# An attention mask carried in the score product's own rows, in a two-layer encoder

## The chip, the cores and the metric

The kernel runs on one core of a Trainium2 chip. The time is in device microseconds (us); it is the median of three runs. One launch computes the whole encoder for one sequence of 512 tokens.

## What is computed

The reference has two layers of the same build. Each adds to the stream x (512 x 1024) half of a SwiGLU feed-forward, then a mixing block, then half of a second feed-forward, and then it is normed. The mixing block has two groups side by side: latent attention with 8 heads, and a causal depthwise convolution of 31 taps over 512 channels; one output projection joins them. The part that the change touches is the attention's scores:

```python
CHUNK, Q_BLOCK, QK_DIM = 64, 128, 96
for i in range(s // Q_BLOCK):                       # 4 blocks of 128 queries
    qs, ks, vs = q[:, :, q0:q0 + 128], k[:, :, :k_end], v[:, :, :k_end]   # k_end = q0 + 128
    scores = einsum('bhqd,bhkd->bhqk', qs, ks) * QK_DIM ** -0.5
    allowed = (arange(k_end) // CHUNK)[None, :] <= ((q0 + arange(128)) // CHUNK)[:, None]
    probs = softmax(where(allowed, scores, -1e30))
    outs.append(einsum('bhqk,bhkd->bqhd', probs, vs))
```

Since a query block sees keys up to its own end only, just one corner of each block has to be masked: the first 64 queries of a block against the last 64 keys.

## The kernel before

**The stages of a layer.** Everything lies transposed, with features on the 128 partitions and the 512 tokens in the free dimension. The two feed-forwards and the projections are products of float32 operands that are split into a high and a low part, three products each (L144 to L146). The mixing block's attention and convolution run together in one stretch, here called the head stage: from 460 to 518 us in layer 0 and from 1370 to 1427 in layer 1 of the profiled execution.

**The attention.** For each head, `turn` (L615) transposes the queries and the keys of 96 features to tiles `qT` and `kT` of 512 columns; ScalarE scales the queries out of PSUM (L625), VectorE the keys (L630). `scores` (L633) makes four score products, one for each block of queries, of 128, 256, 384 and 512 keys (L646); behind each comes a mask product (L647), which adds `mrow` times `mneg` to the last 64 columns: `mrow` and `mneg` are bfloat16 tiles with one row that is not zero, 1 for the first 64 queries and -1e30. Then VectorE takes the maximum of each row (L648) and ScalarE the exponential with its sum (L652). `turn_p` (L656) transposes the probabilities (L667), and VectorE copies two of the three results out of PSUM and ScalarE one (L670). `values` (L673) makes the products with the values (L680). `turn_out` turns a pair of heads (L698).

**Order.** The heads are a pipeline that is written out by `ORDER = "t0s1p3v4o5"`: in each step a head is turned, the one before it makes its scores, and so on; two heads are turned ahead. The final place of an instruction on its engine is set by the framework's scheduler, which models when operands and buffers are there. Each engine then runs its own list in order.

**The convolution.** `CONV = "DAAD"` gives the four channel groups of the convolution to engines: two groups are one VectorE instruction for each tap (`cv`, L734), and in the other two ScalarE makes a tap's product (`pr`, L738) and POOL adds it (`y`, L742). These fill the same stretch as the heads. When all four are done, POOL sums them (L756 to L758) in `t`, and TensorE's product `pm` (L760) takes their mean over the channels. So the mixing block goes on with what is late of the two groups.

**Buffers and loads.** `qT`, `kT` and the probabilities are tiles of a ring of 41 buffers of 128 x 512 (named `r`). Weights are loaded by SP's queue into `raw`, three buffers in turn (L129); a load waits on SP until its buffer is free, and SP runs its list in order. The eight pieces of the output projection `wout` are loaded this way in the head stage: four of them of the kind "sum" (ScalarE makes the negative, and a POOL transfer adds the weights to it, L134 and L135). Behind them stand, on SP, the loads `fr` of the second feed-forward's weights (`wgu`, L253).

Of the kernel before, what the change touches and what calls it, by code (L numbers as in the profile page):

```python
# [6 lines left out]

FP = mybir.dt.float32
FR = mybir.dt.float32r
BF = mybir.dt.bfloat16  # L10
I32 = mybir.dt.int32
AF = mybir.ActivationFunctionType
ALU = mybir.AluOpType
# [2 lines left out]
P = 128  # L16
D = 1024
S = 512
# [4 lines left out]
DN = 64  # L23
DR = 32
DQ = DN + DR
DV = 64
QL = 384
KVL = 256
# [37 lines left out]


@with_exitstack
def encoder_kernel(ctx: ExitStack, tc: tile.TileContext, xT, consts, vecs, rgain, wgu1, wd1,
                   wcv, wql, wkl, wuq, wkv, wout, wgu2, wd2, out):  # L70
    nc = tc.nc
    PSUM = bass.MemoryType.PSUM
    cpool = ctx.enter_context(tc.tile_pool(name="const", bufs=1))
# [8 lines left out]
    def nm(s):  # L82
        uid[0] += 1
        return f"{s}{uid[0]}"

    def slot(dt=FP, w=S):
        return ring.tile([P, w], dt, tag="r", name=nm("r"))

    def tmp(w=S, dt=FP):
        return tmps.tile([P, w], dt, tag="t", name=nm("t"))  # L90

    def bank():
        return psum.tile([P, S], FP, tag="ps", name=nm("ps"))

    def tiny(tag, w, dt=FP):
        return small.tile([P, w], dt, tag=tag, name=nm(tag))

    V, A, G, T = nc.vector, nc.scalar, nc.gpsimd, nc.tensor
# [3 lines left out]
    vec = cpool.tile([P, L, VN], FP, name="vec")  # L102
# [10 lines left out]
    V.memset(minus_half, -0.5)  # L113
    onesm = cpool.tile([P, P], FP, name="onesm")
    V.memset(onesm, 1.0 / CW)
    mrow = cpool.tile([P, P], BF, name="mrow")
    V.memset(mrow, 0.0)
    V.memset(mrow[0:1, 0:64], 1.0)
    mneg = cpool.tile([P, 64], BF, name="mneg")
    V.memset(mneg, 0.0)  # L120
    V.memset(mneg[0:1, :], -1e30)

    def vv(l, name):
        o, w = VOFF[name]
# [309 lines left out]
    def mix_body(kpool, l, gx, norm, done):  # L434
# [27 lines left out]
        ck = kpool.tile([P, NT, KW], FP, tag="ck", name=nm("ck"), bufs=1)  # L462
        q = kpool.tile([P, NT, H, DQ], FP, tag="q", name=nm("q"), bufs=1)
        kn = kpool.tile([P, NT, H, DQ], FP, tag="kn", name=nm("kn"), bufs=1)
        cq, wkl_, sk, ckc, ratio = (tiny(n, NT) for n in ("cq", "wkl", "sk", "ckc", "ratio"))
# [42 lines left out]
        def rope(v, tb, h):  # L508

            nt = v.shape[1]  # L510
            x1, x2 = v[:, :, :, 0:16], v[:, :, :, 16:32]
            m = []
            w = nt * h * 16
            s1, s2 = tmp(), tmp()
            for i, src in enumerate((x1, x2, x1, x2)):
                a = (s1, s2)[i // 2][:, i % 2 * w:(i % 2 + 1) * w]
                a = a.rearrange("p (t h j) -> p t h j", t=nt, h=h)
                V.tensor_tensor(a, src, tb[:, i, :, None, :].to_broadcast([P, nt, h, 16]), ALU.mult)
                m.append(a)
            V.tensor_tensor(x1, m[0], m[1], ALU.subtract)  # L520
            V.tensor_tensor(x2, m[2], m[3], ALU.add)
# [9 lines left out]
        def token_terms():  # L531


            vx = norm.st.ve
            V.tensor_scalar(cq, vx, EPS * EPS * DQ, None, ALU.mult)
            V.scalar_tensor_tensor(cq, stq.sums(), EPS * DQ / QL, cq, ALU.mult, ALU.add)
            V.tensor_scalar(wkl_, vx, EPS, None, ALU.mult)
# [3 lines left out]
            V.tensor_tensor(ckc, ckc, sspe, ALU.mult)  # L541
            V.scalar_tensor_tensor(ckc, ckc, EPS * DQ, wkl_, ALU.add, ALU.mult)
            V.tensor_tensor(ratio, rm, sk, ALU.mult)
            V.tensor_tensor(ratio, ratio, wkl_, ALU.mult)

        def queries():
            wq = [load_w(wuq[l, :, k * 768:(k + 1) * 768], 768, "uq") for k in range(3)]
            for t in range(NT):
# [17 lines left out]
                if t % 2:  # L566
                    rope(q[:, t - 1:t + 1, :, DN:DQ], tabs[0][:, :, t - 1:t + 1], H)
                    if not QFOLD:
# [49 lines left out]
        heads = [{} for _ in range(H)]  # L618

        def turn(h):  # L620
            ps = bank()
            for t in range(NT):
                T.transpose(ps[0:DQ, t * P:(t + 1) * P], q[:, t, h], ident)
            qT = slot()
            A.activation(qT[0:DQ], ps[0:DQ], AF.Copy, scale=gqs[0:DQ])  # L625
            ps = bank()
            for t in range(NT):
                order["turned"] = T.transpose(ps[0:DQ, t * P:(t + 1) * P], kn[:, t, h], ident).ins
            kT = slot()
            V.tensor_scalar(kT[0:DQ], ps[0:DQ], gk, None, ALU.mult)  # L630
            heads[h]["qk"] = qT, kT

        def scores(h):  # L633
            qT, kT = heads[h]["qk"]
            b01, b2, b3 = bank(), bank(), bank()
            if h % 2 == 0:
                heads[h]["sums"] = small.tile([P, NT, 2], FP, tag="sums", name=nm("sums"), bufs=3)
            sums = heads[h - h % 2]["sums"]
            mx = small.tile([P, NT], FP, tag="mx", name=nm("mx"), bufs=3)
            pi = []  # L640
            ps = [slot() for _ in range(3)]
            ps = [ps[0][:, 0:128], ps[0][:, 128:384], ps[1][:, 0:384], ps[2]]
            for i in range(NT):
                n = (i + 1) * P
                o = (b01[:, 0:128], b01[:, 128:384], b2[:, 0:384], b3)[i]
                T.matmul(o, qT[0:DQ, i * P:(i + 1) * P], kT[0:DQ, 0:n], start=True, stop=False)  # L646
                heads[h]["s"] = T.matmul(o[:, n - 64:n], mrow, mneg, start=False, stop=True).ins  # L647
                V.tensor_reduce(mx[:, i:i + 1], o, axis=AX.X, op=ALU.max, negate=True)  # L648
                p = ps[i]
                if QFOLD:  # L650
                    V.tensor_tensor(mx[:, i:i + 1], mx[:, i:i + 1], scqs[i][:, h:h + 1], ALU.mult)
                A.activation(p, o, AF.Exp, bias=mx[:, i:i + 1], scale=scqs[i][:, h:h + 1] if QFOLD else 1.0,  # L652
                             accum_out=sums[:, i, h % 2:h % 2 + 1])
                pi.append(p)
            heads[h]["p"] = pi
# [17 lines left out]
        def values(h):  # L673
# [4 lines left out]
            for t in range(NT):  # L678
                for j in range(t + 1):
                    T.matmul(po[:, t, h % 2], heads[h]["pt"][j][:, (t - j) * P:(t - j + 1) * P],  # L680
                             vs[j][:, h * DV:(h + 1) * DV], start=j == 0, stop=j == t)
            if h % 2 == 0:
# [4 lines left out]
            V.tensor_tensor(o.rearrange("p (t h d) -> p t h d", t=NT, h=2), po,  # L687
                            rs[:, :, :, None].to_broadcast([P, NT, 2, DV]), ALU.mult)
            heads[h]["o"] = o

        def turn_out(h):
# [7 lines left out]
            at.append(split(ps))  # L699

        STAGES = [({"t": turn, "s": scores, "p": turn_p, "v": values, "o": turn_out}[c], int(d)) for c, d in zip(ORDER[::2], ORDER[1::2])]

        wv = load_w(wkv[l, 1], WC, "uk")
        for h in range(AHEAD):
            turn(h)
# [8 lines left out]
        with tc.issue_after(order["gate"]):  # L714
            scores(0)
        for step in range(H + 6):
            for stage, lag in STAGES:
                h = step - lag
# [7 lines left out]
        for c in range(4):  # L726
# [4 lines left out]
            for k in range(CK - 2, -1, -1):  # L731
                s = CK - 1 - k
# [41 lines left out]
        for c in range(4):  # L774
            z = tmp()
            V.tensor_tensor(z, ys[c], pr, ALU.mult)
            s = tmp()
# [54 lines left out]
    for l in range(L):  # L832
# [46 lines left out]
        else:  # L879
# [8 lines left out]
            for m in (2, 3, 4, 0, 5, 6, 1, 7):  # L888
                o = slot()
# [87 lines left out]
```

## Time and profile before

The time is 1840.56 us, the median of 1840.35, 1840.56 and 1844.12. The profile is of one execution.

| | |
|---|---|
| the profiled execution's time, its span | 1841.61 us, 1839.5 us |
| busy: TensorE (PE), its weight loads (PEld) | 1809.6 us (98%), 1619.6 us (88%) |
| busy: VectorE (DVE), ScalarE (ACT), GpSimd (POOL) | 1356.9 us (74%), 932.8 us (51%), 338.7 us (18%) |
| chain of work that ended last | PE 87%, DVE 5%, ACT 4%, POOL 2% |
| transfers | 175.72 MB, mean 96 GB/s |
| mask products (L647) | 64, half of them in each layer's head stage |

A row of the timeline has the start and the busy time in us, the engine, the line, the operation and its tiles (out <- in), its shapes, and in brackets how long the engine was idle before it and what ended that. A row of the busy time by stretches has, after the stretch and its length, the busy time and number of instructions of PE, PEld, DVE, ACT and POOL, then the clock that TensorE was granted (1.00 is full speed), the share of the transfer engines and what they moved in GB/s. A row of the transfers has the queue, the size and the median time from issue to landing. "span" is the time from the first to the last instruction on the core.

### The profile page before, as it was taken

The page shows a single profiled execution, that of the slowest core. Times are in us where ns is not written, and L with a number is a line of the kernel's source. Part 1 is how long each engine was busy: PE and PEld are TensorE (multiplying, and loading weights), DVE is VectorE, ACT ScalarE, POOL GpSimd, SP SyncE. Part 2 cuts the span into 40 slices and gives each one's busy share as a digit, 9 for nine tenths or more (in the row PEclk, how much of TensorE's full clock was granted, in tenths as well). Part 3 has the DMA queues.
Part 4 walks back from the last instruction along what each step waited for, and adds up shares of the span by engine and source line. Part 5 has one row for each costly group of instructions (what it writes and reads, how often), then busy time and mean ns, then how long its engine had stood idle before and what let it go on. Part 6 is the DMA issues. An engine that isn't in the chain of part 4 may idle for free.

```text
span 1839.5 us, 27876 instructions
## 1 busy us (share of the span) xinstructions
PE 1809.6 (98%) x11248; PEld 1619.6 (88%) x11248; DVE 1356.9 (74%) x1772; ACT 932.8 (51%) x1464; POOL 338.7 (18%) x238
## 2 busy tenths in 40 slices
PE   8999999999999999999999999999999999999997
PEld 6898989888788898989888999998978788989895
DVE  7976767589956986858779676765998669767673
ACT  5453535457953553535634435354778434535352
POOL 1000000248943000000410000002589400000002
PEclk9999999999999999999999999999999999999998
DMA  5242422325123142422512424133250322414221
GB/s 220 74 136 61 143 65 81 115 78 138 32 82 96 50 144 65 133 66 92 177 50 69 141 65 142 56 95 108 79 149 1 126 64 64 152 55 145 62 87 63
DMA packets 55569, 175.72 MB, mean 96 GB/s; under 512 B 6160, under 2 KB 6544, under 8 KB 55440
## 3 DMA queue, kind: packets, MB, share of 16 engines
q1 hardware_dynamic: 53856, 169.37, 29.4%
q0 software_dynamic: 1152, 4.19, 1.3%
q8 instruction: 88, 1.44, 0.3%
q10 hardware_dynamic: 432, 0.38, 0.1%
q14 instruction: 41, 0.34, 0.1%
HBM read 171.82 MB, written 2.10 MB: 95 GB/s over the span
## 4 chain that ended last, share of the span: by engine, by line
PE 87%; DVE 5%; ACT 4%; POOL 2%; issue 2%; DMA 0%; DVEq 0%; SPq 0%; POOLq 0%; ACTq 0%
PE ps L144 28%; PE ps L146 28%; PE ps L145 27%; PE ps L680 1%; POOL y L742 1%; ACT pr L738 1%; DVE r L293 1%; PE ps L646 1%; DVE t L298 1%; ACT r L652 1%; DVE cv L734 1%; DVE wl L137 1%; PE ps L667 1%; ACT wh L131 1%; PE ps L187 1%
## 5 line engine op out<-in xcount | busy, mean ns | idle before, releaser
L144 PE MATMUL ps<-r,wh 128*128 128x256 f32 (+1 forms) x3280 | 1052.6, 327 | 7.7 <-ACT wh L131 6.7
L145 PE MATMUL ps<-r,wh 128*128 128x256 f32 (+1 forms) x3280 | 1059.0, 324 | 0.0
L146 PE MATMUL ps<-r,wl 128*128 128x256 f32 (+1 forms) x3280 | 1051.7, 324 | 3.8 <-DVE wl L137 1.9
L144 PEld LDWEIGHTS ps<-r,wh 128*128 128x128 f32 x3280 | 620.3, 190 | 63.3 <-ACT wh L131 7.8
L146 PEld LDWEIGHTS ps<-r,wl 128*128 128x128 f32 x3280 | 621.2, 190 | 56.7 <-DVE wl L137 4.4
L145 PEld LDWEIGHTS ps<-r,wh 128*128 128x128 f32 x3280 | 624.5, 190 | 52.0 <-issue 2.4
L233 ACT CAST wh<-fr 128x1024 fp32r<-128x1024 f32 x216 | 226.9, 1051 | 316.7 <-PE ps L145 232.9
L131 ACT CAST wh<-raw 128x768 fp32r<-128x768 f32 (+4 forms) x214 | 187.2, 882 | 334.6 <-PE ps L145 163.2
L235 DVE TENSOR_TENSOR wl<-fr,wh 128x1024 fp32r<-128x1024 f32 x216 | 263.6, 1221 | 77.2 <-ACT wh L233 74.0
L180 POOL TENSOR_TENSOR acc<-acc,t 128x512 f32<-128x512 f32 x46 | 79.2, 1729 | 1297.0 <-ACT t L176 1296.3
L137 DVE TENSOR_TENSOR wl<-raw,wh 128x768 fp32r<-128x768 f32 (+4 forms) x198 | 207.9, 1054 | 121.3 <-ACT wh L131 120.2
L417 DVE SCALAR_TENSOR_TENSOR x<-ps,x 128x512 f32<-128x512 f32 x128 | 87.5, 686 | 120.1 <-PE ps L146 120.1
L742 POOL TENSOR_TENSOR y<-y,pr 128x511 f32<-128x511 f32 (+14 forms) x120 | 157.1, 1310 | 54.0 <-ACT pr L738 46.5
L734 DVE SCALAR_TENSOR_TENSOR cv<-r,vec,cv 128x511 f32<-128x511 f32 (+14 forms) x120 | 87.7, 731 | 3.4 <-ACT cv L730 2.1
L738 ACT ACTIVATE pr<-r,vec 128x511 f32<-128x511 f32 (+14 forms) x120 | 84.2, 726 | 11.6 <-POOL y L742 11.6
L233 ACT CAST wh<-raw 128x1024 fp32r<-128x1024 f32 x36 | 37.7, 1047 | 69.6 <-PE ps L145 69.6
L150 ACT CAST r<-t 128x512 fp32r<-128x512 f32 x96 | 55.6, 618 | 33.5 <-DVE t L270 20.7
L151 DVE TENSOR_TENSOR r<-t,r 128x512 fp32r<-128x512 f32 x96 | 64.6, 686 | 10.2 <-ACT r L150 10.2
L235 DVE TENSOR_TENSOR wl<-raw,wh 128x1024 fp32r<-128x1024 f32 x36 | 44.1, 1225 | 30.2 <-ACT wh L233 30.2
L346 DVE TENSOR_TENSOR raw<-fr,fr 128x1024 f32<-128x1024 f32 x36 | 44.0, 1222 | 14.3 <-DMA fr<-in_wgu 14.2
L144 PE MATMUL ps<-wh,r 128*128 128x288 f32 (+2 forms) x144 | 48.5, 337 | 0.7 <-ACT r L625 0.7
L157 DVE SCALAR_TENSOR_TENSOR r<-x,vec,r 128x512 fp32r<-128x512 f32 x40 | 45.6, 1149 | 4.6 <-ACT r L156 4.6
(171 smaller groups left out, 1602.4 us busy)
## 6 DMA issues: line engine op xcount, KB each, us to landing
fr<-in_wgu SPq DMA_DIRECT2D x144, 512.0 KB, 3.6
raw<-in_wd SPq DMA_DIRECT2D x96, 384.0 KB, 3.2
raw<-in_wgu SPq DMA_DIRECT2D x32, 512.0 KB, 3.6
raw<-in_wd SPq DMA_DIRECT2D x32, 256.0 KB, 2.6
raw<-in_wcv SPq DMA_DIRECT2D x16, 512.0 KB, 3.6
raw<-in_wout SPq DMA_DIRECT2D x16, 512.0 KB, 4.1
wl<-in_wout POOLq DMA_DIRECT2D x8, 512.0 KB, 6.9
raw<-in_wql SPq DMA_DIRECT2D x6, 512.0 KB, 3.5
```

Of the source, the lines that this page charges most:

```text
L131: A.copy(hi[:, :w], raw[:, :w])
L137: (G if kind in POOLW.split() else V).tensor_tensor(lo[:, :w], raw[:, :w], hi[:, :w].bitcast(FP), ALU.subtract)
L144: T.matmul(o, lh, rh, start=first, stop=False, skip_group_check=free)
L145: T.matmul(o, lh, rl, start=False, stop=False, skip_group_check=free)
L146: T.matmul(o, ll, rh, start=False, stop=last, skip_group_check=free)
L180: (eng or (V if last else G)).tensor_tensor(self.acc, self.acc, sq, ALU.add)
L233: A.copy(hi[:, :w], src[:, :w])
L235: V.tensor_tensor(lo[:, :w], src[:, :w], hi[:, :w].bitcast(FP), ALU.subtract)
L417: V.scalar_tensor_tensor(x[:, m, :], pd, 0.5, x[:, m, :], ALU.mult, ALU.add)
L734: V.scalar_tensor_tensor(acc[:, s:], u[c][:, :S - s], tap(k), acc[:, s:], ALU.mult, ALU.add)
L738: A.activation(pr[:, s:], u[c][:, :S - s], AF.Copy, scale=tap(k))
L742: order["conv"] = G.tensor_tensor(acc[:, s:], acc[:, s:], pr[:, s:], ALU.add).ins
```

## The change

The mask becomes part of the score product. `qT` and `kT` get four more rows, 96 to 99, one for each block of 128 tokens. Row 96 + j of the queries is 1 for the first 64 tokens of block j and 0 elsewhere; row 96 + j of the keys is -1e30 for the last 64 tokens of block j and 0 elsewhere. Their product is -1e30 just where the corner of block j is masked. Both sets of rows come with a new input, `masks`, of 2 x 4 x 512 numbers, and are written into each head's two tiles by transfers on SP's queue: 2 of 8 KB for each head, 16 for each layer. The mask products and the two bfloat16 tiles with their four memsets go.

```diff
+DM = DQ + S // P
...
-    mrow = cpool.tile([P, P], BF, name="mrow")
-    V.memset(mrow, 0.0)
-    V.memset(mrow[0:1, 0:64], 1.0)
-    mneg = cpool.tile([P, 64], BF, name="mneg")
-    V.memset(mneg, 0.0)
-    V.memset(mneg[0:1, :], -1e30)
...
             ps = bank()
             for t in range(NT):
                 T.transpose(ps[0:DQ, t * P:(t + 1) * P], q[:, t, h], ident)
-            qT = slot()
+            qT, kT = slot(), slot()
+            nc.sync.dma_start(out=qT[DQ:DM], in_=masks[0])
+            nc.sync.dma_start(out=kT[DQ:DM], in_=masks[1])
             A.activation(qT[0:DQ], ps[0:DQ], AF.Copy, scale=gqs[0:DQ])
...
-            kT = slot()
             V.tensor_scalar(kT[0:DQ], ps[0:DQ], gk, None, ALU.mult)
...
-                T.matmul(o, qT[0:DQ, i * P:(i + 1) * P], kT[0:DQ, 0:n], start=True, stop=False)
-                heads[h]["s"] = T.matmul(o[:, n - 64:n], mrow, mneg, start=False, stop=True).ins
+                heads[h]["s"] = T.matmul(o, qT[0:DM, i * P:(i + 1) * P], kT[0:DM, 0:n], start=True, stop=True).ins
...
+    block, chunk = np.divmod(np.arange(S), P)[0], np.arange(S) % P // 64
+    own = block[None, :] == np.arange(S // P)[:, None]
+    masks = np.stack([own & (chunk == 0), own & (chunk == 1)]).astype(f32)
+    masks[1] *= f32(-1e30)
```

The scheduler places the new transfers and moves some of the work around them. On SP, in layer 0, the last loads of `wout` ahead of the loads `fr` stand like this before:

```order
L129 DMA raw_5045<-in_wout 128x1024
L129 DMA raw_5481<-in_wout 128x1024
L129 DMA raw_5499<-in_wout 128x1024
L129 DMA raw_5579<-in_wout 128x1024
L253 DMA fr_6212<-in_wgu 128x1024
```

After the change (lines of the file are six lower here), the same place reads:

```order
L123 DMA raw_5459<-in_wout 128x1024
L123 DMA raw_5477<-in_wout 128x1024
L619 DMA r_4397<-in_masks 4x512
L620 DMA r_4398<-in_masks 4x512
L619 DMA r_4413<-in_masks 4x512
L620 DMA r_4414<-in_masks 4x512
L123 DMA raw_5557<-in_wout 128x1024
L619 DMA r_4487<-in_masks 4x512
L620 DMA r_4488<-in_masks 4x512
L619 DMA r_4522<-in_masks 4x512
```

The masks of heads 0 and 1 stand between the sixth and the seventh load of `wout`, those of heads 2 to 7 behind the seventh and ahead of the loads `fr`. In layer 1 the order is the same.

On VectorE, in layer 0 at head 2, the stretch with the maxima of head 2 (`mx_4543`), the copies of head 0's probabilities (`r_4564`, `r_4578`), the convolution's taps (`cv_5267`) and head 3's keys (`r_4594`) is before:

```order
L734 SCALAR_TENSOR_TENSOR cv_5267<-r_4388,vec,cv_5267 128x505
L648 TENSOR_REDUCE mx_4543<-ps_4541 128x1
L734 SCALAR_TENSOR_TENSOR cv_5267<-r_4388,vec,cv_5267 128x504
L648 TENSOR_REDUCE mx_4543<-ps_4539 128x1
L670 COPY r_4564<-ps_4563 128x512
L685 RECIPROCAL rs_4716<-sums_4467 128x8
L670 COPY r_4578<-ps_4577 128x256
L734 SCALAR_TENSOR_TENSOR cv_5267<-r_4388,vec,cv_5267 128x503
L630 TENSOR_SCALAR r_4594<-ps_4589,vec 96x512
```

And after (`mx_4537`, `r_4554`, `r_4568`, `cv_5245` and `r_4578` in the same roles):

```order
L642 TENSOR_REDUCE mx_4537<-ps_4535 128x1
L728 SCALAR_TENSOR_TENSOR cv_5245<-r_4382,vec,cv_5245 128x505
L664 COPY r_4554<-ps_4553 128x512
L664 COPY r_4568<-ps_4567 128x256
L642 TENSOR_REDUCE mx_4537<-ps_4533 128x1
L728 SCALAR_TENSOR_TENSOR cv_5245<-r_4382,vec,cv_5245 128x504
L679 RECIPROCAL rs_4702<-sums_4465 128x8
L625 TENSOR_SCALAR r_4578<-ps_4582,vec 96x512
```

Both copies and the keys of head 3 stand one tap earlier, and the copies ahead of a maximum that they stood behind.

On ScalarE, in layer 1, the taps of 509 and 508 columns (`pr`), the copy of probabilities (L670) and the scaled queries (L625) stand like this before:

```order
L652 ACTIVATE r_13477,sums_13474<-ps_13472,mx_13475 128x384
L652 ACTIVATE r_13478,sums_13474<-ps_13473,mx_13475 128x512
L670 COPY r_13503<-ps_13502 128x512
L738 ACTIVATE pr_14115<-r_13250,vec 128x509
L625 ACTIVATE r_13519<-ps_13514,gqs_13322 96x512
L652 ACTIVATE r_13476,sums_13474<-ps_13471,mx_13475 128x256
L738 ACTIVATE pr_14118<-r_13250,vec 128x508
L738 ACTIVATE pr_14121<-r_13250,vec 128x507
```

And after (L646 are the exponentials, L664 the copy, L621 the queries, L732 the taps):

```order
L646 ACTIVATE r_13455,sums_13452<-ps_13450,mx_13453 128x384
L646 ACTIVATE r_13456,sums_13452<-ps_13451,mx_13453 128x512
L664 COPY r_13477<-ps_13476 128x512
L621 ACTIVATE r_13493<-ps_13488,gqs_13300 96x512
L732 ACTIVATE pr_14077<-r_13228,vec 128x509
L732 ACTIVATE pr_14080<-r_13228,vec 128x508
L646 ACTIVATE r_13454,sums_13452<-ps_13449,mx_13453 128x256
L732 ACTIVATE pr_14083<-r_13228,vec 128x507
```

The tap of 509 columns stands behind the queries' eviction, and the tap of 508 ahead of an exponential. On TensorE the mask products are gone, and a few transposes and score products of neighbouring heads change places; POOL's order is the same.

More of the change, by code (lines that the diff above doesn't have):

```diff
@@ L9 @@
 FR = mybir.dt.float32r
-BF = mybir.dt.bfloat16
 I32 = mybir.dt.int32
@@ L68, in encoder_kernel @@
 @with_exitstack
-def encoder_kernel(ctx: ExitStack, tc: tile.TileContext, xT, consts, vecs, rgain, wgu1, wd1,
+def encoder_kernel(ctx: ExitStack, tc: tile.TileContext, xT, consts, masks, vecs, rgain, wgu1, wd1,
                    wcv, wql, wkl, wuq, wkv, wout, wgu2, wd2, out):
@@ L956 @@
     consts[:, CID:CID + P] = np.eye(P, dtype=f32)
+    block, chunk = np.divmod(np.arange(S), P)[0], np.arange(S) % P // 64
+    own = block[None, :] == np.arange(S // P)[:, None]
+    masks = np.stack([own & (chunk == 0), own & (chunk == 1)]).astype(f32)
+    masks[1] *= f32(-1e30)
     arrays = {
         "xT": a["x"][0].T.reshape(KD, P, S),
-        "consts": consts, "vecs": vec, "rgain": rgain,
+        "consts": consts, "masks": masks, "vecs": vec, "rgain": rgain,
         "wgu1": quarters(a["ffn1_w_gate"], a["ffn1_w_up"]), "wd1": cols(a["ffn1_w_down"]),
```

## The prediction

> **What bounds the kernel now.** I read the page first, then the busy time by stretches of the head stage, then PE's and the other engines' timelines there, and last the answers on single lines.
>
> ```profile
> span 1839.5 us, 27876 instructions
> PE 1809.6 (98%) x11248; PEld 1619.6 (88%) x11248; DVE 1356.9 (74%) x1772; ACT 932.8 (51%) x1464; POOL 338.7 (18%) x238
> PE 87%; DVE 5%; ACT 4%; POOL 2%; issue 2%; DMA 0%; DVEq 0%; SPq 0%; POOLq 0%; ACTq 0%
> L647 PE MATMUL ps<-mneg,mrow x64: 193/194/258, 460.1 to 1415.9; 128*128 128x64 bf16 x64
> 460.00:470.00 10.00, 8.79 (x42) 5.66 (x41) 8.62 (x17) 10.00 (x23) 9.53 (x9) 0.83 0.67 142
> 480.00:490.00 10.00, 10.00 (x76) 8.40 (x76) 9.96 (x21) 9.74 (x23) 9.37 (x9) 1.00 0.01 2
> 500.00:510.00 10.00, 10.00 (x81) 8.77 (x80) 9.06 (x18) 9.99 (x25) 9.37 (x9) 1.00 0.01 2
> 510.00:520.00 10.00, 9.22 (x76) 8.52 (x76) 4.17 (x9) 3.30 (x6) 6.70 (x6) 1.00 0.01 2
> ```
>
> The kernel is PE's: 98% busy and 87% of the chain of waits. The 64 mask products (32 in each layer) stand only in the two head stages, near 460 to 518 and 1370 to 1427 us. The stretches (PE, PEld, DVE, ACT, POOL busy, then the granted clock) say that this stage has no single limit: PE, ACT, DVE and POOL are all over 9 of 10 us until about 510, and only then PE works alone. So work that leaves PE here is worth its PE time only where no other engine is the next to be late.
>
> **What leaves PE.** The masks' own price, from the timelines of PE and of its weight loads:
>
> ```profile
> 482.52 0.39 PE L646 MATMUL ps<-r,r 96*128 96x128 f32 x2
> 482.75 0.20 PE L647 MATMUL ps<-mneg,mrow 128*128 128x64 bf16 x1
> 482.78 0.89 PE L646 MATMUL ps<-r,r 96*128 96x384 f32 x2
> 501.69 0.47 PE L646 MATMUL ps<-r,r 96*128 96x128 f32 x2
> 501.99 0.19 PE L647 MATMUL ps<-mneg,mrow 128*128 128x64 bf16 x1
> 482.64 0.10 PEld L647 LDWEIGHTS <-mrow 128*128 128x128 bf16 x1
> 482.75 0.30 PEld L646 LDWEIGHTS ps<-r,r 96*128 96x128 f32 x2
> ```
>
> From its start to the next one's a mask takes 482.78 - 482.75 = 0.03 us. But the same 128-column score product takes 482.75 - 482.52 = 0.23 us behind a transpose and 501.99 - 501.69 = 0.30 behind a mask, since its weights begin to load only when the mask starts (482.75) and so short a product can't cover that load. A mask ahead of a score product costs 0.03 + 0.07 = 0.10 us. In the program's order 36 of the 64 stand so; the other 28 stand ahead of transposes and value products, which I estimate at 0.05 (between 0.03 and 0.10, nearer the first, since those load weights at every step anyway). Sum: 36 x 0.10 + 28 x 0.05 = 5.0 us of PE, 0.08 each. [...] A score product over 100 rows rather than 96 I cost at nothing: value products over 128 rows and transposes over 128 or 96 run in the same stage with nothing to tell them apart; bounds 0 and 0.04 us a product, both small. Four memsets leave DVE at the start, where it waits for the first weights: nothing.
>
> **What comes: 32 transfers of 8 KB on SP's queue.** The trace has no transfer so small; what bounds them is what they queue behind.
>
> ```profile
> 455.06 0.33 SPq L129 DMA_DIRECT2D raw<-in_wout  x1
> raw<-in_wout SPq DMA_DIRECT2D x1, 512.0 KB, 4.2
> 463.79 0.33 SPq L129 DMA_DIRECT2D raw<-in_wout  x1
> raw<-in_wout SPq DMA_DIRECT2D x1, 512.0 KB, 6.6
> 1373.83 0.33 SPq L129 DMA_DIRECT2D raw<-in_wout  x1
> raw<-in_wout SPq DMA_DIRECT2D x1, 512.0 KB, 6.3
> DMA to landing us min/median/max: 3.6/5.6/7.2
> raw<-in_wd SPq DMA_DIRECT2D x32, 256.0 KB, 2.6
> 459.92 0.27 PE L646 MATMUL ps<-r,r 96*128 96x128 f32 x1
> 469.35 0.50 PE L646 MATMUL ps<-r,r 96*128 96x128 f32 x2
> 469.93 0.29 DVE L648 TENSOR_REDUCE mx<-ps 128x1 f32<-128x128 f32 x1 [0.71 <-PE ps L647]
> 475.29 0.46 PE L646 MATMUL ps<-r,r 96*128 96x128 f32 x2 [0.54 <-DVE r L670]
> 1377.85 0.39 PE L646 MATMUL ps<-r,r 96*128 96x128 f32 x2
> 1378.41 0.28 DVE L648 TENSOR_REDUCE mx<-ps 128x1 f32<-128x128 f32 x1
> ```
>
> The row 3.6/5.6/7.2 is the burst of five 512 KB loads that SP issues at 531.6: each lands behind the one before, so I take SP's queue as one line. Heads 0 and 1's masks stand behind the transfer of 455.06, which lands at 459.3; head 0's first product is at 459.92, so no stall there. The masks of heads 2 to 7 stand behind the next one. It lands at 463.79 + 6.6 = 470.4, and head 2's first product runs at 469.35: PE waits 1.0 us. In layer 1 it lands at 1380.1 against 1377.85: 2.3 us, of which a 256-column product moved ahead of it fills 0.4. Bounds: the fastest load, 2.6 us, would land them at 466.8 and 1376.9 and nothing would wait; 0.6 us behind the big one the stalls are 1.6 and 2.8. I take the landing itself, since the burst is the nearest row. [...] From head 3 on the masks' buffers are free heads ahead, and nothing waits. SP's queue holds no other work until the loads after the stage.
>
> **What is late next.** Behind head 2's product DVE waits too, since its reduce (469.93, 1378.41) stands in DVE's order. In layer 0 head 3 waits for DVE's copy (the 0.54 at 475.29). In the new order that copy stands one convolution step and one reduce earlier, about 1 us, which pays for the stall, and the 20 masks from head 3 on then save 20 x 0.08 = 1.6 us. But PE then meets POOL:
>
> ```profile
> 477.59 35.50 POOL L742 TENSOR_TENSOR y<-y,pr 128x508 f32<-128x508 f32 x27 [1.10 <-ACT pr L738]
> 515.74 1.27 POOL L758 TENSOR_TENSOR t<-t,r 128x512 f32<-128x512 f32 x1
> 518.61 1.02 PE L760 MATMUL ps<-t,onesm 128*128 128x512 f32 x2
> 1387.63 35.47 POOL L742 TENSOR_TENSOR y<-y,pr 128x508 f32<-128x508 f32 x27 [0.35 <-ACT pr L738]
> 1425.76 1.26 POOL L758 TENSOR_TENSOR t<-t,r 128x512 f32<-128x512 f32 x1
> 1427.43 1.02 PE L760 MATMUL ps<-t,onesm 128*128 128x512 f32 x2
> 1382.19 1.02 DVE L670 COPY r<-ps 128x512 f32<-128x512 f32 x2
> 1383.89 0.39 PE L646 MATMUL ps<-r,r 96*128 96x128 f32 x2
> ```
>
> POOL adds the convolution's taps without a break from 477.59 (1387.63) to the sum at L758, which PE's L760 reads. L758 ends at 517.01 in layer 0, 1.6 us before L760, and at 1427.02 in layer 1, 0.4 before. PE can gain no more than that unless POOL ends sooner, and ACT, which feeds POOL, is full. In layer 0 I therefore count -1.2 us of the 1.6 (some goes to ACT's full stretch). In layer 1 DVE's reduce moves from 1378.41 to about 1380.6 and the copies that follow (1382.19 to 1383.2) to about 1385; head 3 starts some 1.2 us after 1383.89, the 1.6 us of saved masks just pay for it, and POOL's 0.4 caps what is left; ACT's new order hands POOL the 509 tap one eviction later, about 0.25. Layer 1: +0.2. **Sum:** -1.2 + 0.2 = -1.0 us.
>
> The profiled execution took 1841.61 us, 2.1 of it outside the span, and the median of the three runs, 1840.56, is 1.05 below. On the median's scale the sum is 1839.6. Bounds: layer 0 between -1.9 (the whole gap to POOL, and its 508 tap earlier) and +0.5 (stall 1.6, half of it not paid back), layer 1 between -0.4 and +1.7: 1838.3 to 1842.8.
>
> **Rivals.**
> *PE alone decides.* If masks land in time and POOL ends sooner, all 5.0 us come: 1835.6. For it: PE's 10.00 of 10 in three stretches. Against: POOL's unbroken rows of 35.5 us and ACT's 10.00. Chance 0.10.
> *Head 2's stall is carried to the end (slower).* Place: the first product of head 2. If its masks land 0.6 us behind the big load, DVE's reduce comes at 471.3 rather than 469.93 (+1.4) and at 1381 rather than 1378.41 (+2.4 with the time to multiply). DVE, at 9 to 10 of 10 afterwards, can't catch up, so what PE saves ends as waiting: +3.8, 1844.4. With a stretch of half clock it is worse: the clock of 0.83 over 460 to 470 is 1.7 us of PE lost after gaps of under 1 us each, and such a stretch in layer 1 makes 1846.1; I take 1845.2. It decides once DVE has not made good its lateness by head 3. For it: DVE's full stretches. Against: the copies' new place, and PE's slack at the tail (510 to 520, where DVE is at 4.17). [...] Chance 0.20.
> *The change buys less than it says.* If the 0.07 stays (another weight load takes the mask's place) or 100 rows cost 0.04 more a product, PE saves 1.9 us or less, the stalls of about 1 and 2 us are not paid, and the sum is +1: 1841.6. Chance 0.05.
>
> **How the numbers follow.** The forecast, 1839.6, has 0.65. A measurement of this kernel can tell about 0.2%, 3.7 us, from no change. The forecast and the third rival lie within that: 0.70 same; faster 0.10; slower 0.20. The range goes from 1837.4, some way from the forecast's own low end towards the first rival, since POOL's end may itself move, up to the slower rival's 1845.2: a part of each of these two rivals is left out, about 0.18 in all.
>
> **What would show it.** After: no L647, score products back to back with the pair of 128 columns at 0.23; PE and DVE idle for 1 and 2 us at head 2's first product, ended by the mask transfer; the L760 product closer behind POOL's L758 in layer 0, at once behind it in layer 1; the rest of the kernel unmoved. I am wrong if head 2 doesn't wait, if POOL's last sum itself moves by more than a microsecond, or if PE's tail stays ahead of POOL.

## The result, and the profile after

The changed kernel takes 1847.51 us (median of 6 runs, 1846.05 to 1849.8) against 1840.49 for the kernel before on the same chip: 7.0 us slower, ratio 1.0036 with a 95% interval of 1.0026 to 1.0046. The forecast was 1839.6, with a range up to 1845.2. The span and the busy time by stretches of the kernel after (PE, PEld, DVE, ACT and POOL busy, then the granted clock), and under them two stretches of the kernel before:

```profile
span 1844.9 us, 27825 instructions
460.00:470.00 10.00, 5.42 (x27) 3.07 (x25) 7.20 (x14) 10.00 (x25) 9.15 (x9) 1.00 0.55 119
470.00:480.00 10.00, 9.56 (x47) 6.62 (x48) 7.94 (x17) 8.45 (x22) 6.35 (x6) 0.83 0.02 5
1380.00:1390.00 10.00, 6.37 (x23) 4.61 (x23) 5.04 (x12) 7.51 (x21) 6.15 (x5) 0.66 0.19 53
```

```profile
470.00:480.00 10.00, 9.46 (x63) 6.86 (x62) 10.00 (x21) 10.00 (x28) 7.79 (x7) 1.00 0.00 0
1380.00:1390.00 10.00, 9.66 (x69) 7.52 (x69) 9.65 (x19) 10.00 (x27) 8.01 (x7) 1.00 0.00 0
```

Around head 2, PE is busy for 5.42 of 10 us in layer 0 (8.79 before), and the clock behind it is down: 0.83 and, in layer 1, 0.66, where it was 1.00. POOL is at 6.35 and 6.15 there, against 7.79 and 8.01 before. The timelines of SP's queue, PE, DVE and POOL there:

```profile
462.67 0.36 SPq L123 DMA_DIRECT2D raw<-in_wout  x1
463.07 0.32 SPq L619 DMA_DIRECT2D r<-in_masks  x1
466.20 0.60 PE L624 MATMUL ps<-cst,kn 128*96 128x128 f32 x4
470.44 3.98 PE L641 MATMUL ps<-r,r 100*128 100x128 f32 x8 [3.64 <-ACT r L621]
470.94 0.29 DVE L642 TENSOR_REDUCE mx<-ps 128x1 f32<-128x128 f32 x1 [3.63 <-PE ps L641]
472.41 3.97 POOL L736 TENSOR_TENSOR y<-y,pr 128x511 f32<-128x511 f32 x3 [1.82 <-ACT pr L732]
1375.61 0.35 SPq L123 DMA_DIRECT2D raw<-in_wout  x1
1379.33 0.70 PE L641 MATMUL ps<-r,r 100*128 100x256 f32 x2
1383.65 3.75 PE L641 MATMUL ps<-r,r 100*128 100x128 f32 x6 [3.63 <-DMA r<-in_masks]
1384.45 0.29 DVE L642 TENSOR_REDUCE mx<-ps 128x1 f32<-128x128 f32 x1 [3.97 <-PE ps L641]
```

PE is done with head 3's transposes at 466.80 and starts head 2's first product at 470.44; in layer 1 the pause is from 1380.03 to 1383.65. In layer 0 the row names ScalarE as what ended the wait, but that instruction is not an operand of head 2, and in a second profile of the changed kernel (again, below) the row of the same wait names the masks' transfer. The trace holds no landing of its own for these transfers. I take the end of the wait for it: 7.8 us after the load of `wout` ahead of them was issued (470.44 - 462.67), and 8.0 in layer 1 (1383.65 - 1375.61).

What sets the time of the next stage is POOL's last sum and TensorE's mean behind it. POOL's waits in the head stage, layer 0 and layer 1 (us in total, times, longest), with layer 1's first score product and, for the kernel after, the ends of the stages; the kernel before comes first:

```profile
POOL y L742 <- ACT pr L738: 1.9, 2, 1.1
POOL y L742 <- ACT pr L738: 2.4, 5, 0.9
1370.41 0.39 PE L646 MATMUL ps<-r,r 96*128 96x128 f32 x2
```

```profile
POOL y L736 <- ACT pr L732: 5.0, 4, 1.8
POOL y L736 <- ACT pr L732: 6.1, 7, 2.9
517.54 1.27 POOL L752 TENSOR_TENSOR t<-t,r 128x512 f32<-128x512 f32 x1
518.87 1.13 PE L754 MATMUL ps<-t,onesm 128*128 128x512 f32 x2
1372.65 1.53 PE L641 MATMUL ps<-r,r 100*128 100x128 f32 x5 [0.32 <-DMA r<-in_masks]
1431.19 1.26 POOL L752 TENSOR_TENSOR t<-t,r 128x512 f32<-128x512 f32 x1
1432.51 1.13 PE L754 MATMUL ps<-t,onesm 128*128 128x512 f32 x2 [0.35 <-POOL t L752]
```

POOL waits 4.3 us for ScalarE's taps before and 11.1 after. That these 6.8 us more are near the 7.0 that were measured is chance: the two profiled executions are only 5.1 us apart (1846.72 and 1841.61). The rows tell where time was lost. The mean's product of layer 0 starts 0.3 us later than before (518.87 against 518.61), the first score product of layer 1 2.2 us later (1372.65 against 1370.41), and the mean's product of layer 1, which follows POOL's sum (ends at 1432.45, before at 1427.02) at once, 5.1 us later (1432.51 against 1427.43). So the head stage of layer 1 loses 2.8 us.

The other two steps are mixed with half-clock stretches that don't come from the masks. The kernel before has one of its own in layer 0's head stage (3.4 us from 466.18, about 1.7 us of PE's work), which hides part of the loss there; and most of the 2.0 us lost between the two head stages is one at 993.35 in the changed kernel. Its second profile has none at 993; in it the same three starts are 1.6, 2.4 and 4.7 us later than before.

### The profile page after: what moved, and what is told of

Same layout as the page of the kernel before. It is cut to its first block, busy times and chain, and to the rows that moved or that the text cites. A ratio compares the mean times of both kernels' runs of the same rounds, so it can differ in the third digit from the quotient of the medians.

```text
span 1844.9 us, 27825 instructions
## 1 busy us (share of the span) xinstructions
PE 1808.2 (98%) x11184; PEld 1619.0 (88%) x11184; DVE 1356.7 (74%) x1768; ACT 934.1 (51%) x1464; POOL 337.6 (18%) x238
## 4 chain that ended last, share of the span: by engine, by line
PE 84%; DVE 7%; POOL 3%; ACT 3%; issue 2%; DMA 1%; SPq 0%; DVEq 0%; POOLq 0%; ACTq 0%
PE ps L138 27%; PE ps L140 27%; PE ps L139 26%; DVE cv L728 2%; POOL y L736 1%; DVE r L287 1%; PE ps L641 1%; DVE wl L131 1%; PE ps L674 1%; ACT pr L732 1%; DVE t L292 1%; ACT wh L125 1%; PE ps L181 0%; PE ps L661 0%; DVE mx L642 0%
## 5 line engine op out<-in xcount | busy, mean ns | idle before, releaser
L732 ACT ACTIVATE pr<-r,vec 128x511 f32<-128x511 f32 (+14 forms) x120 | 83.3, 721 | 9.3 <-POOL y L736 9.3
L641 PE MATMUL ps<-r,r 100*128 100x384 f32 (+3 forms) x128 | 44.7, 473 | 9.4 <-DMA r<-in_masks 3.9
```

Of the source, the lines that this page charges most:

```text
L732: A.activation(pr[:, s:], u[c][:, :S - s], AF.Copy, scale=tap(k))
```

## The experiments

Each kernel was timed in turn with the kernel before on one chip; ratios are to that.

**1. Masks of heads 2 and 3 ahead of the load (early4).** The tiles of heads 0 to 3 are taken, and their transfers issued, ahead of the head loop:

```diff
+        for h in range(4):
+            heads[h]["qk"] = masked()      # two slots, two mask transfers
...
-            qT, kT = slot(), slot()
+            qT, kT = heads[h]["qk"] if h < 4 else masked()
```

> The changed kernel, with the two tiles of heads 0 to 3 taken and their mask transfers issued ahead of the head loop, so that on SP the masks of heads 2 and 3 stand ahead of the seventh load of wout instead of behind it. Theory A (the loss is the stall of PE at head 2, 3.6 us in each layer, and the half clock that follows it): the stall goes, no half-clock window after it, and the time falls from 1847.5 to between 1838 and 1841. Theory B (the loss is in what the transfers, the 100 rows or the new order do over the whole stage): the time stays within 1.5 us of 1847.5.

1840.42 us, ratio 0.9995 (0.9986 to 1.0004). On SP these eight transfers now stand between the sixth and the seventh load of `wout`, no pause of over 1.3 us is left on PE in the stage, and the loss is gone. So it lies in where head 2's masks stand on SP's queue.

**2. The transfers alone (dmas).** The kernel before, with 32 transfers into rows that nothing reads:

```diff
+            nc.sync.dma_start(out=qT[DQ:DM], in_=masks[0])
+            nc.sync.dma_start(out=kT[DQ:DM], in_=masks[1])
```

> The kernel before, mask products kept, with the 32 transfers added into rows 96 to 99 that no product reads. Theory A (the loss is the wait for the transfers at head 2): nobody waits, so 1840.5 within 1.0 us. Theory B (the transfers themselves cost, on SP's queue, on the ring's buffers or by the order that the scheduler makes of them): 1844 to 1848.

1840.32 us, ratio 0.9997 (0.9988 to 1.0005): the transfers cost nothing when nobody waits for them.

**3. No mask at all (nomask), and 4. the mask rows turned along with the queries and keys (fold).** In fold the token-side tiles carry the four columns, filled by ten small memsets in each layer:

```diff
-        q = kpool.tile([P, NT, H, DQ], ...)
+        q = kpool.tile([P, NT, H, DM], ...)
+            V.memset(a[:, :, :, DQ:DM], 0.0)
+            for t in range(NT):
+                V.memset(a[ps, t, :, DQ + t], value)     # 1.0 on q, -1e30 on kn
-                T.transpose(ps[0:DQ, ...], q[:, t, h], ident)
+                T.transpose(ps[0:DM, ...], q[:, t, h], ident)
```

> The changed kernel without transfers and without any mask: score products over 96 rows, the mask is left out. It is what the change could bring at most. Theory A1 (PE meets POOL's last sum soon, which moves little): 1838 to 1840. Theory A2 (PE alone decides in the head stage): 1835 to 1836.5, 5 us below the kernel before.

> The mask in the score product's rows, without transfers: the token-side tiles q and kn get four more columns a head, filled by five memsets each and layer, and the transposes turn 100 rows instead of 96, so that the evictions write the mask rows. Theory A (only the transfers' landing costs): as without a mask, within 0.7 us of that kernel, 1836 to 1840. Theory B (100 rows or the order cost): 2 us or more above the kernel without a mask, 1842 or more.

1841.55 us, ratio 0.9997 (0.9989 to 1.0006), and 1841.51, ratio 0.9998 (0.9990 to 1.0007), beside 1841.65 for the kernel before on this chip. So the 64 mask products are worth nothing that can be measured, even when all that replaces them is free, and 100 rows cost as little as 96. The ends of the stage, nomask in layer 0 and fold in layer 1:

```profile
517.43 1.69 PE L752 MATMUL ps<-t,onesm 128*128 128x512 f32 x2 [0.31 <-POOL t L750]
```

```profile
1424.94 1.13 PE L756 MATMUL ps<-t,onesm 128*128 128x512 f32 x2 [0.99 <-POOL t L754]
```

PE has run out of work and waits for POOL's sum. In nomask the product behind that wait takes 1.69 us rather than 1.02, and the clock is 0.89 over 510 to 520 us, where it is 1.00 in the kernel before and in fold: here the work that left PE made it idle, and the clock took about 0.7 us of the gain back. My expectations' absolute times were at least 1.5 us too low here; 1.2 of that is the kernel before, which was itself slower on this chip, so the ratio is what counts.

**5. The wait alone (dmawait).** Mask products kept, transfers of zeros, and products over 100 rows, so that they wait:

```diff
-                T.matmul(o, qT[0:DQ, i * P:(i + 1) * P], kT[0:DQ, 0:n], start=True, stop=False)
+                T.matmul(o, qT[0:DM, i * P:(i + 1) * P], kT[0:DM, 0:n], start=True, stop=False)
```

> The kernel before, mask products kept, with the 32 transfers (of zeros) and score products over 100 rows, so that head 2 waits for its transfers as in the changed kernel, and no PE work is saved. Theory A (the wait at head 2 is the whole loss, and the mask products saved bring under 1 us, since POOL's last sum decides): 1846 to 1849, like the changed kernel. Rival (the saved products do bring their 5 us, and the waits cost 12): 1850 to 1853.

1850.61 us, ratio 1.0053 (1.0041 to 1.0066): 9.3 us lost, against 7.0 with the masks gone. It lies between what the two theories gave: with a wait in the stage the saved products seem to bring some 2 of their 5 us, since then PE's stream is late. The two intervals of the ratios overlap (1.0041 against 1.0046), so this difference is not certain.

**6. Every mask twice (twice).**

```diff
+                T.matmul(o[:, n - 64:n], mrow, mneg, start=False, stop=False)
                 heads[h]["s"] = T.matmul(o[:, n - 64:n], mrow, mneg, start=False, stop=True).ins
```

> The kernel before with every mask product made twice: 64 more products, which prices one. If a mask costs PE 0.08 us, as my prediction had it, PE gets 5 us more work and the end moves by that less the 2.0 us of gap between POOL's last sum and the mean's product: 1843 to 1844. If it costs 0.03 us, 1.9 us in all: 1840.5 to 1841.5. In both the trace shows the price at the same places.

1842.56 us, ratio 1.0008 (1.0000 to 1.0017), 1.2 more than 1841.32, between the two forecasts. The timeline of PE, and under it one of the changed kernel:

```profile
501.78 0.19 PE L647 MATMUL ps<-mneg,mrow 128*128 128x64 bf16 x1
501.82 0.19 PE L648 MATMUL ps<-mneg,mrow 128*128 128x64 bf16 x1
501.84 0.47 PE L646 MATMUL ps<-r,r 96*128 96x128 f32 x2
502.15 0.19 PE L647 MATMUL ps<-mneg,mrow 128*128 128x64 bf16 x1
```

```profile
501.37 1.47 PE L641 MATMUL ps<-r,r 100*128 100x256 f32 x6
```

A second mask adds 0.03 us (501.82 - 501.78, rounded; 33 ns over all 64), 2.1 in all. The product behind still takes 0.31 (502.15 - 501.84), against 0.23 without a mask ahead of it: its weights are late once, not twice. So this run prices the mask's own 0.03, not the 0.07 that I put on top of it. The trace of the changed kernel does: its row holds the products of 256, 128 and 384 keys of a head, 1.47 us from start to end. In the kernel before the same three, with two masks between them, start at 501.17 and end at 502.91, 1.74 us: 0.27 for two masks, so the 0.10 apiece was not too high.

**7. Two taps fewer on ScalarE and POOL, with and without masks (before_taps, nomask_taps).**

```diff
-            for k in range(CK - 2, -1, -1):
+            for k in range(CK - 2, -1 if kind == "D" else 1, -1):
```

> The kernel before with the last two taps of the two ScalarE-and-POOL channel groups left out: 4 adds (5.2 us of POOL) and 4 products of ScalarE (2.9 us) less in each layer. Theory A (POOL's sum and PE's stream end within 2 us of each other before): little comes of it, since PE is next: 1837 to 1840.

> The same two taps left out, and the mask left out too. Theory A (POOL's last sum is what ate the saved mask products): with POOL out of the way the mask products show, 3 to 5 us below the kernel with fewer taps and masks: 1833 to 1836. Rival (the head stage's PE is held by ScalarE's and VectorE's evictions, not by POOL's end): less than 1.5 us below it.

1840.07 us, ratio 0.9998 (0.9989 to 1.0007), and 1839.73, ratio 0.9992 (0.9983 to 1.0001). My theory A failed: with POOL done early, leaving the masks out still brings under 1.5 us. End of the stage in nomask_taps, and the waits of its score products, under those of before_taps:

```profile
509.79 1.27 POOL L750 TENSOR_TENSOR t<-t,r 128x512 f32<-128x512 f32 x1
516.49 1.02 PE L752 MATMUL ps<-t,onesm 128*128 128x512 f32 x2
```

```profile
PEld ps L646 <- ACT r L652: 2.9, 4, 1.2
```

```profile
PEld ps L639 <- ACT r L644: 5.9, 6, 1.8
```

POOL ends 5.4 us ahead of the mean's product, and still PE ends its stream in layer 0 hardly sooner (516.49 against 517.06 in before_taps): what it saves on masks it waits out on ScalarE's exponentials (5.9 us rather than 2.9), which free the banks that the next score products need. There are two walls behind PE here, ScalarE in the stage's first 20 us (10.00 of 10 busy over 460 to 470 and 470 to 480 in both) and POOL at its end.

**8. POOL's three sums on VectorE (before_sumv, fold_sumv).**

```diff
-        G.tensor_tensor(ysum, ys[0], ys[1], ALU.add)
-        G.tensor_tensor(ysum, ysum, ys[2], ALU.add)
-        (G if YP else V).tensor_tensor(ysum, ysum, ys[3], ALU.add)
+        V.tensor_tensor(ysum, ys[0], ys[1], ALU.add)      # and the other two alike
```

> The kernel before with the three sums of the convolution's channel groups on VectorE instead of POOL (0.7 us each instead of 1.27). Between POOL's last sum and the mean's product lie 1.6 and 0.4 us: PE's own stream is late too, so no more than 0.5 us come of it: 1840 to 1841.5.

> The kernel with folded mask columns, with the same three sums on VectorE. There PE waits for POOL's last sum, 0.6 and 1.0 us: this goes, 1.6 us in all, and the time is 1838.5 to 1840.5, below both kernels. If ScalarE and VectorE, not POOL's end, hold PE: no change from the folded kernel, 1841 to 1842.

1849.25 us, ratio 1.0048 (1.0036 to 1.0060), and 1846.88, ratio 1.0037 (1.0025 to 1.0049): both slower, a miss. The first one's timeline in layer 0:

```profile
518.89 0.68 DVE L758 TENSOR_TENSOR t<-t,r 128x512 f32<-128x512 f32 x1
519.72 1.82 PE L760 MATMUL ps<-t,onesm 128*128 128x512 f32 x2 [2.09 <-DVE t L758]
```

The scheduler put the sums behind the last head's output on VectorE, so that PE waits 2.1 us for them; and the product behind that wait takes 1.82 instead of 1.02: PE is at half speed there, the next products start 0.43 us apart up to 523.04 and 0.23 from 523.43 on. Two waits of 2.1 us, one in each layer, stand here against 7.7 us lost: a sign that a wait of PE can cost more than its length.

**9. PE kept at work during the wait (warm, warm14).** Products of the identity with itself go into the bank that head 2's first product starts anew:

```diff
+                if h == 2 and i == 0:
+                    for _ in range(32):                   # 14 in warm14
+                        T.matmul(b01[:, 0:128], ident, ident, start=True, stop=True)
```

> The changed kernel with 32 products of the identity with itself (128 columns, about 3.5 us in all) ahead of head 2's first score product in each layer, into the bank that this product starts anew: PE works in the time in which it otherwise waits for the masks. Theory A (part of the loss is the half clock that follows PE's idle 3.6 us): the wait stays as long, no half-clock window follows it, and the time falls by 2 to 5 us from 1847.5, to 1843 to 1845.5. Theory B (the half clock costs nothing, since other engines hold the stage; the wait alone is the loss): 1847.5 within 1 us.

1849.01 us, ratio 1.0041 (1.0029 to 1.0053). The filler was too long, a product taking 0.23 us: if the masks land 8 us behind the load as above, head 2 started 3 to 5 us after them. No half clock follows the filler (1.00 over each 10 us from 480 to 530 and from 1370 to 1440), so holding PE that much longer costs 7.5 us by lateness alone, and this run doesn't tell the theories apart. With 14:

> The filler once more, with 14 products in place of 32: in the run before, one took 0.23 us instead of 0.11, so that the 32 held PE 3 to 4 us beyond the masks' landing, and no half clock followed. 14 x 0.23 = 3.2 us, which ends before the landing. Theory A (the loss is the wait of 3.6 us in each layer and, on top, half-clock windows that follow it, less 2.5 us of saved masks): the wait stays, no window of half clock follows it, and the time is 1842 to 1845. Theory B (the clock costs nothing in the end): 1847.5 within 1 us.

1840.85 us, ratio 1.0002 (0.9993 to 1.0011): the whole loss is gone, more than theory A said, though head 2 starts as late as in the changed kernel. But here the scheduler had also put three taps ahead of head 2's maximum on VectorE, and ScalarE's taps stood otherwise. The next two take that back.

**10. The same with VectorE's order (warmhold) and ScalarE's too (warmhold2).**

```diff
+                    with tc.issue_after(heads[2]["mx"]) if c == 3 and s >= 6 else nullcontext():
                         V.scalar_tensor_tensor(acc[:, s:], ...)       # VectorE's tap
...
+                    with tc.issue_after(heads[2]["exp"]) if c == 2 else nullcontext():
                         A.activation(pr[:, s:], ...)                  # ScalarE's tap, warmhold2 only
```

> The kernel with 14 filling products once more, with VectorE's taps of channel group 3 from the 506-column one on held behind head 2's first maximum in the order, as the changed kernel has them: VectorE idles while the masks are on their way, and TensorE does not. Theory C (what costs is VectorE's idle time behind the wait, the clock adds little): 1844.5 to 1847.5. Theory D (what costs is the half clock behind TensorE's idle time; VectorE makes its 3 us good): 1840 to 1842.5, as with the filling products alone.

> The kernel before it (filling products, VectorE's taps held behind head 2's first maximum) with ScalarE's taps of channel group 2 also held behind head 2's first exponential, so that ScalarE too waits with its taps as in the changed kernel, and POOL waits for them. Theory D (the half clock behind TensorE's idle time is most of the loss): POOL's waits for ScalarE grow by the one wait of 1.2 to 1.8 us at head 2 in each layer and the time is 1840.5 to 1843. Theory E (the order of ScalarE, with the wait, starves POOL, and the clock adds little): 1845 to 1848.

> The changed kernel itself once more, for the comparison on this chip and for a second profile of it. The half-clock windows behind head 2's wait in both layers are in this profile too if they belong to the wait; the one at 993 us, behind a gap of 1.4 us that every kernel has, is there only if the clock's windows fall so. Time 1846 to 1849.8, as before.

1840.01 us, ratio 0.9999 (0.9990 to 1.0008); 1841.18, ratio 0.9999 (0.9990 to 1.0008); and the changed kernel once more, beside warmhold on one chip: 1847.67, ratio 1.0038 (1.0025 to 1.0052). In the second profile of the changed kernel each of the two waits is followed by 6.8 us at half clock, and the window near 993 is missing. Theory D holds. PE's timeline, the waits of POOL in both layers and the clock in warmhold2:

```profile
467.78 0.60 PE L624 MATMUL ps<-cst,kn 128*96 128x128 f32 x4
468.22 2.62 PE L641 MATMUL ps<-cst 128*128 128x128 f32 x22
470.67 0.60 PE L644 MATMUL ps<-r,r 100*128 100x256 f32 x2
471.11 0.83 PE L641 MATMUL ps<-cst 128*128 128x128 f32 x6
471.78 1.89 PE L644 MATMUL ps<-r,r 100*128 100x128 f32 x6
467.00:474.00 7.00, 7.00 (x51) 5.85 (x50) 4.79 (x10) 6.85 (x19) 5.19 (x6) 1.00 0.45 123
1378.00:1390.00 12.00, 11.65 (x81) 9.41 (x78) 9.28 (x19) 11.54 (x31) 9.64 (x9) 1.00 0.22 61
POOL y L743 <- ACT pr L739: 1.5, 1, 1.5
POOL y L743 <- ACT pr L739: 2.3, 5, 0.7
```

From the transposes' end (468.38) to head 2's first product (471.78) PE does 3.4 us of filling and one product of head 1; DVE is busy for 4.79 of 7 us: it waits 2.2 us ahead of head 2's first maximum, and 2.7 in layer 1, against 3.6 and 4.0 in the changed kernel (3.1 in layer 0 of warmhold). The last 0.5 and 1.3 us of VectorE's wait are not in this test. The clock stays at 1.00, POOL waits 3.8 us in all instead of 11.1, and nothing is lost. In layer 0 one difference of order is left: head 1's last score product stands ahead of head 2's, where the changed kernel has it behind; in layer 1 both have it ahead.

Of these kernels none is measurably faster than the kernel before.

## Why the prediction was wrong, point by point

- **Masks in SP's queue behind the load: the place was right, the time luck in part.** early4 shows that the loss hangs on this place. The landing in layer 0 was put at 470.4, and PE starts at 470.44; but the load was issued 1.1 us earlier than before (462.67 against 463.79), and the masks came 7.8 us behind its issue where I had put its own 6.6. In layer 1 it was 8.0 rather than 6.3. I named "behind the big one" as a bound with 0.6 us, which no run shows; it was 1.2 and 1.7. Why the masks come so much later than the load alone did before stays open.
- **The stall's length: the step that failed first.** It was taken as landing minus the time at which head 2's product ran before, 1.0 us, and 2.3 less 0.4 of filling; it was 3.6 in both. In layer 1 PE came as early in its stage as before (7.4 us behind the first score product in both), and the late landing makes the difference. In layer 0 PE also arrived earlier (466.80, where the product had started at 469.35 before): the old start stood behind a stretch at half clock (from 466.18, the 0.83 that I quoted for another purpose), 1.6 us of delay that the new kernel doesn't have.
- **What the stall costs: the step that failed most.** In the sum, head 2's stall was paid for by DVE's earlier copy and the saved masks: -1.2 us for layer 0 and +0.2 for layer 1, with nothing for the clock behind it, though a rival carried that. Measured, layer 1's head stage alone lost 2.8 us in the profiled execution, and the kernel 7.0 in the median. The runs show that a stall as long costs nothing while PE works (warm14, warmhold, warmhold2), and 7 us when it idles. In the changed kernel's trace 3.4 and 6.8 us at half clock follow the two waits, 5.1 us of PE's work; in its second profile 6.8 and 6.8. The rest of the way, exponentials late, ScalarE's taps behind them late, POOL waiting, is read from the traces and not tried apart.
- **The sign that was named came true.** POOL's last sum moved by more than a microsecond, 1.8 us in layer 0 (518.81 against 517.01) and 5.4 in layer 1.
- **The clock: left out of the sum.** That no half clock follows the stalls was an estimate of mine that no row bore out. The profile before has 3.4 us at half clock from 466.18, with 1.2 us of idle PE in the 3.4 us ahead of it and no gap there over 0.80; the two stalls became 3.6 us long. In the rows below PE is idle for between 1.2 us and all of the 3.41 us ahead of a half clock.
- **The slower rival.** It had the place right, and 1845.2 against 1847.5, at a chance of 0.20. Its carrier was VectorE's lateness, with a half clock only on top; warmhold leaves VectorE idle for 3.1 us in layer 0 and loses nothing. (Its +2.4 should read 2.6: 1381 - 1378.41.)
- **PE's saving and the cap by POOL: right in size, incomplete in cause.** Without the wait the change brings 0.02 to 0.05% (early4, fold, nomask; each interval includes no change), which the sum of -1.0 us fits, and the trace bears out 0.10 us for a mask between two score products. PE does wait for POOL's last sum there. But POOL is not the only wall (nomask_taps), and it is no fixed wall either: it moves with ScalarE, which is how a wait at head 2 reaches the end.
- **Nothing for 100 rows, the transfers themselves and the memsets: right within the noise** (fold, dmas).

## What to carry to other kernels

Before a transfer takes the place of cheap work, find out on which queue it will stand, behind what, and where its consumer really arrives once the work is gone; a start time from the old trace is not that arrival. A wait of TensorE that the rest of the program can absorb may still cost, by the clock behind it: 3.6 us of idling were followed here by 3.4 to 6.8 us at half clock, just where several engines are full. Filling the wait with products that nobody reads is a test that tells the wait and the clock apart, once the order of the other engines is held. And where three engines are near 10 of 10, as here, work removed from the fourth can be worth nothing until they are relieved too.

## What the runs showed of the hardware

The stretches at half clock in the rows below last 3.41 or 6.83 us. In the changed kernel they start at 471.11, 993.35 and 1382.46 us, 522.24 and 389.11 us apart; divided by 153 and by 114, both give 3.413. In its second profile they start at 470.62 and 1381.98, 911.36 us apart, which divided by 267 is 3.413 too. Whether that holds for other kernels is not shown here. The busy time of the 3.41 us ahead of such a stretch and of the stretch itself, in the kernel after, in the kernel before, in fold and in the second profile of the changed kernel; near 990 us in the kernel before and in fold no half clock follows:

```profile
467.69:471.11 3.42, 0.67 (x4) 0.68 (x5) 0.17 (x1) 2.66 (x8) 2.74 (x3) 1.00 0.28 84
471.11:474.52 3.41, 3.41 (x8) 1.59 (x7) 2.29 (x6) 3.26 (x9) 2.03 (x2) 0.50 0.04 10
989.93:993.35 3.42, 1.53 (x9) 0.92 (x7) 2.78 (x3) 3.42 (x4) 0.00 (x0) 1.00 0.00 0
993.35:996.76 3.41, 3.18 (x15) 3.18 (x16) 3.41 (x4) 0.14 (x1) 0.00 (x0) 0.50 0.56 156
1379.05:1382.46 3.41, 0.97 (x6) 0.47 (x4) 1.44 (x3) 3.41 (x11) 2.67 (x3) 1.00 0.80 221
1382.46:1385.87 3.41, 2.22 (x5) 1.60 (x6) 1.42 (x3) 2.37 (x8) 1.55 (x2) 0.50 0.02 5
1385.87:1389.29 3.42, 3.42 (x12) 2.32 (x11) 2.50 (x6) 2.19 (x6) 2.54 (x2) 0.50 0.02 5
```

```profile
462.76:466.18 3.42, 2.21 (x12) 1.31 (x11) 3.42 (x8) 3.42 (x9) 3.34 (x4) 1.00 0.41 53
466.18:469.59 3.41, 3.41 (x13) 2.13 (x13) 2.37 (x5) 3.41 (x12) 3.17 (x4) 0.50 1.00 253
991.83:995.24 3.41, 2.09 (x17) 2.09 (x18) 3.41 (x4) 1.23 (x2) 0.00 (x0) 1.00 0.31 80
995.24:998.65 3.41, 3.41 (x30) 3.41 (x30) 2.49 (x3) 1.57 (x3) 0.00 (x0) 1.00 0.78 252
```

```profile
989.54:992.95 3.41, 1.98 (x16) 1.99 (x17) 3.41 (x4) 1.29 (x2) 0.00 (x0) 1.00 0.31 59
992.95:996.36 3.41, 3.41 (x31) 3.41 (x30) 2.60 (x3) 1.54 (x2) 0.00 (x0) 1.00 0.74 249
```

```profile
467.21:470.62 3.41, 0.00 (x0) 0.00 (x1) 0.00 (x0) 3.02 (x9) 3.09 (x3) 1.00 0.38 107
470.62:474.04 3.42, 3.39 (x7) 2.27 (x8) 2.39 (x5) 2.16 (x6) 1.12 (x1) 0.50 0.05 14
474.04:477.45 3.41, 3.41 (x13) 2.63 (x12) 2.07 (x5) 2.51 (x6) 2.69 (x3) 0.50 0.00 0
1378.57:1381.98 3.41, 1.31 (x10) 0.82 (x7) 1.97 (x4) 3.41 (x12) 2.69 (x3) 1.00 0.81 228
1381.98:1388.81 6.83, 5.39 (x15) 3.67 (x16) 3.66 (x8) 4.75 (x13) 4.42 (x4) 0.50 0.01 3
```

In the changed kernel's first profile, 2.75 us of idle PE ahead (467.69) and 1.9 (989.93) were followed by 3.4 us at half clock, 2.4 (1379.05) by 6.8; in the second, 3.4 (467.21) and 2.1 (1378.57) by 6.8. With 1.2 us it happened (before, 462.76), with 1.3 (before, 991.83) and 1.4 (fold) it did not: in these rows the idle time alone does not decide it. PE has the same gap of 1.44 us in the kernel before (ends at 993.15) and in the changed kernel (993.58), and of the two the clock halves at it only in the changed kernel. The 3.4 and 6.8 us that follow the two waits at head 2 in one profile, and 6.8 and 6.8 in the other, could be part of why the changed kernel's runs spread over 3.7 us, but this was not tried.
